# Row sums inverted by exp(-log) on ScalarE and a Newton step on VectorE, in place of VectorE's reciprocal

## The chip, the cores and the metric

The kernel runs on one core of one Trainium2 chip. A core has five engines with a queue each: TensorE (PE, matrix products; PEld is its weight load), VectorE (DVE), ScalarE (ACT), GpSimd (POOL) and SyncE (SP, which issues the DMAs here). An engine takes its own instructions strictly in order. The metric is the device time of one launch in microseconds (us), the median of several runs.

## The reference

One layer of a hybrid encoder is applied with the same weights to a group of 2048 tokens and one of 512. What matters here is the attention: 8 query heads of width 64 share 2 key/value heads, and each query attends to all tokens of its own group.

```python
def one_block(q_blk):
    s = jnp.einsum('bkgqd,btkd->bkgqt', q_blk, k).astype(jnp.float32) * scale
    p = jax.nn.softmax(s, axis=-1)
    return jnp.einsum('bkgqt,btkd->bkgqd', p.astype(v.dtype), v)
...
mixed = jnp.concatenate([o_attn * jax.nn.silu(a_gate), o_gla * jax.nn.silu(l_gate)], axis=-1)
h = h + mixed @ w_out
```

Beside it stands a gated linear attention (two directions), then an output projection, a per-layer gate (a sigmoid of a projection of the normalised result times a projected embedding), and a final RMS norm. The softmax divides each row of exponentials by its sum; that division is what the change touches.

## The kernel before, in words

Four stages follow each other on the core. Stage 1 normalises the input and projects q, k, v. Stage 2 is the linear attention; it uses Exp and Ln on ScalarE. Stage 3 is the softmax attention and the gates. Stage 4 is the output projection, the per-layer gate and the final norm.

In stage 3 the tokens lie in five chunks of 512 (chunks 0 to 3 are the long group, chunk 4 the short one). An item of work is one chunk of queries and one head: 40 items, `items` in line 860. `head` (line 783) walks over the keys in tiles of 128: 16 tiles, or 4 for chunk 4. For each tile TensorE makes the scores into a PSUM tile `pss` (lines 816 and 817; two and later three buffers), ScalarE takes the exponential into `p` (line 818), and for each two tiles ScalarE casts `p` to half precision (`phi`, line 825) and VectorE makes the rest (`plo`, line 827); TensorE then multiplies both by v into `po` (lines 797 and 805) and sums them over keys into `pz` (line 801). At the end of a head ScalarE copies `pz` to `acc` and two instructions bring `po` to `ou` (lines 833 to 837).

Other work is woven in by hand. After each exponential of line 818, `pull` (line 926) advances five generators by a counted number of steps, inside `tc.issue_after(e.ins)`, which queues what a step issues on ScalarE behind that exponential; on the other engines the planner orders by program order and readiness. The generators are the row maxima of later items (`maxima`: products `px` of line 762, VectorE reductions of line 768, two PSUM buffers), the end of stage 2 (`fin`), the gates (`gates`: 24 products `pg` of line 728 into one PSUM buffer, a Tanh on ScalarE in line 732, then line 733 on VectorE), the row sums (`normalise`) and the stores (`combine`, `store_mixed`).

`normalise` (line 840) runs once for every two heads, 20 times. It sums `acc` over partitions with four products into a PSUM tile `pn` (line 845; the tile shares the two buffers of `px`), inverts it into `rs`, and GpSimd multiplies `ou` by `rs` (line 851). Each `yield` is one step, so each of its instructions lands behind the exponential of another key tile. `combine` then multiplies by the gate, and `store_mixed` splits and stores the result to DRAM for stage 4, which reads the chunks in order of tokens.

ScalarE has table loads among its instructions. Line 56 asks for a table by the name `natural_log_exp_and_others` at the start. The program writes out no other load; the trace holds one more, just before the first Tanh of line 732.

Of the kernel before, what the change touches and what calls it, by code (L numbers as in the profile page):

```python
# [9 lines left out]
F32 = mybir.dt.float32  # L10
# [4 lines left out]
AF = mybir.ActivationFunctionType  # L15
ALU = mybir.AluOpType
# [4 lines left out]
P = 128  # L21
# [648 lines left out]
def stage3(net, s, fin=iter(()), top=None, tail=None):  # L670
    nc, tc, d = net.nc, net.tc, net.d
    with ExitStack() as ctx:
# [4 lines left out]
        rp = pool("s3r", 1)  # L677
# [162 lines left out]
        def normalise(ou, accs):  # L840
            for _ in range(2):
                yield
            pn = ps_n_tile()
            for b in range(2):
                nc.tensor.matmul(pn[b * 64:b * 64 + 64], lhsT=two, rhs=accs[b], start=True, stop=True)  # L845
            rs = rp.tile([P, 512], F32, name="rs")
            for i in range(4):
                cs = slice(i * P, (i + 1) * P)
                nc.vector.reciprocal(rs[:, cs], pn[:, cs])  # L849
                yield  # L850
            nc.gpsimd.tensor_tensor(ou, ou, rs, ALU.mult)  # L851

        def combine(c, j, ou):
# [10 lines left out]
        nt = [4 if c == 4 else 16 for c, h in items]  # L864
# [20 lines left out]
        def all_sums():  # L885
            while True:
                if pairs:
                    c, j, ou, accs = pairs.pop(0)
                    yield from normalise(ou, accs)
                    waiting.append((c, j, ou))  # L890
                else:
                    yield True
# [302 lines left out]
```

## Time and profile before

| | |
|---|---|
| median of 3 runs | 2087.77 us (2084.49 to 2088.56) |
| profiled execution, its own time | 2088.21 us |
| its span in the profile | 2086.5 us |
| mean granted TensorE clock | 0.987 |
| reciprocals of line 849 | 80, first start 672.5 us, last start 1557.2 us |
| Tanh of line 732 | 40, first start 682.2 us, last start 1515.1 us |
| table loads | 2 |

The profile is of one execution. Busy time of an engine is the time in which it ran an instruction; TensorE's is drawn out by pipelining, as the ends of matrix products are modelled. Idle time before an instruction is put down to the instruction that ended the wait. The chain of waits is followed back from the end: at each step to what released the instruction, or to its predecessor on its engine. Stage 3 with gates runs from about 690 to 1520 us.

### The profile page before, as it was taken

What the parts mean: (1) busy time and instruction counts of PE and PEld (TensorE: products, weight loads), DVE (VectorE), ACT (ScalarE), POOL (GpSimd) and SP (SyncE); (2) the same over time, 40 slices, a digit from 0 to 9 for tenths busy, and PEclk for the clock granted to TensorE, in tenths of its full rate; (3) what the DMA queues carried; (4) which work ended last, traced back from release to release, by engine and by line L of the source; (5) the groups of instructions that cost most, each with busy time, mean ns of one, the idle gap of its engine ahead of it and who ended that gap; (6) DMA issues with size and microseconds to landing.
All of it is one profiled execution on the core that took longest, in us unless ns stands there. A gap on an engine that the chain in (4) does not pass through costs nothing.

```text
span 2086.5 us, 29717 instructions
## 1 busy us (share of the span) xinstructions
PE 2004.7 (96%) x11174; PEld 1321.1 (63%) x11174; DVE 1332.6 (64%) x2242; ACT 1181.5 (57%) x2048; POOL 356.5 (17%) x292
## 2 busy tenths in 40 slices
PE   8999999999979999999999999999989999999998
PEld 7788887777754444444444444444437888888886
DVE  7555444665678889899889989988874222222223
ACT  5343233555558888788878878878883222222222
POOL 2434431000430011011011011100120111111111
PEclk9999999999999999999999999999999999999999
DMA  8887445666775225333333422522236222222220
GB/s 269 241 254 209 134 128 167 202 203 199 227 229 188 79 97 171 106 112 108 114 112 128 143 80 94 177 68 93 80 115 187 86 86 86 86 86 86 81 66 33
DMA packets 251360, 282.23 MB, mean 135 GB/s; under 512 B 41872, under 2 KB 180976, under 8 KB 246096
## 3 DMA queue, kind: packets, MB, share of 16 engines
q1 hardware_dynamic: 251072, 279.80, 43.0%
q8 instruction: 88, 1.44, 0.3%
q0 software_dynamic: 144, 0.52, 0.1%
q14 instruction: 56, 0.46, 0.1%
HBM read 189.64 MB, written 90.64 MB: 134 GB/s over the span
## 4 chain that ended last, share of the span: by engine, by line
PE 79%; DVE 8%; ACT 7%; DMA 3%; issue 2%; POOL 1%; SPq 0%; DVEq 0%; POOLq 0%; ACTq 0%
PE pm L108 38%; PE pg L728 9%; PE po L805 5%; PE px L762 4%; PE pss L816 4%; PE pss L817 4%; ACT p L818 3%; PE po L797 3%; PE pp L108 3%; PE pz L801 2%; DVE plo L827 2%; DVE mx L768 2%; ACT phi L825 2%; PE pn L845 1%; PE pt L1080 1%
## 5 line engine op out<-in xcount | busy, mean ns | idle before, releaser
L818 ACT ACTIVATE p<-pss,lnp,qk_scale 128x512 f32<-128x512 f32 x544 | 407.3, 781 | 113.4 <-PE pss L817 100.9
L768 DVE TENSOR_REDUCE mx<-px 128x1 f32<-128x512 f32 x544 | 357.0, 682 | 68.1 <-PE px L762 66.6
L728 PE MATMUL pg<-xt,wg 128*128 128x512 f32 x960 | 376.4, 484 | 1.1 <-DVE g L733 0.9
L827 DVE TENSOR_TENSOR plo<-p,phi 128x1024 f16<-128x1024 f32 x272 | 338.9, 1248 | 34.6 <-ACT phi L825 32.8
L825 ACT CAST phi<-p 128x1024 f16<-128x1024 f32 x270 | 283.2, 1049 | 5.6 <-PE po L805 0.9
L728 PEld LDWEIGHTS pg<-xt,wg 128*128 128x128 f32 x960 | 181.7, 190 | 69.1 <-issue 6.7
L816 PE MATMUL pss<-qa,ka 128*128 128x512 f16 x544 | 208.8, 385 | 11.1 <-ACT p L818 10.2
L762 PE MATMUL px<-ka,qa 128*128 128x512 f16 x544 | 201.0, 384 | 10.3 <-DVE mx L768 6.3
L817 PE MATMUL pss<-qb,kb 66*128 66x512 f16 x544 | 206.4, 383 | 0.3 <-ACT qb L781 0.3
L1128 DVE SCALAR_TENSOR_TENSOR th<-th,pp 128x512 f32<-128x512 f32 (+1 forms) x41 | 27.7, 675 | 190.0 <-ACT th L1127 190.0
L805 PE MATMUL po<-phi,v 128*128 128x512 f16 x544 | 142.5, 385 | 0.0
L108 PE MATMUL pm<-xt,wlqk 128*128 128x512 f32 x480 | 120.4, 410 | 7.8 <-DMA xt<-scr_xt 6.3
L816 PEld LDWEIGHTS <-ka 128*128 128x128 f16 x544 | 52.8, 97 | 107.0 <-issue 83.7
L1081 ACT CAST hT<-pt 128x512 fp32r<-128x512 f32 x40 | 23.5, 587 | 169.7 <-PE pt L1080 169.7
L108 PEld LDWEIGHTS pm<-xt,wlqk 128*128 128x128 f32 x480 | 94.3, 199 | 30.0 <-DMA xt<-scr_xt 7.5
L108 PE MATMUL pm<-wq_h,xt 128*128 128x512 f32 x320 | 103.2, 403 | 4.5 <-ACT xt L203 4.3
L762 PEld LDWEIGHTS <-qa 128*128 128x128 f16 x544 | 52.4, 98 | 83.9 <-issue 41.9
L1127 ACT ACTIVATE th<-pm,rh 128x512 f32<-128x512 f32 (+1 forms) x41 | 27.9, 680 | 133.8 <-PE pm L108 133.8
L108 PE MATMUL pm<-wpg0h,hT 128*128 128x512 f32 x320 | 101.0, 396 | 0.1
L108 PE MATMUL pm<-wo0h,mx 128*128 128x512 f32 x320 | 100.5, 395 | 0.0
L108 PE MATMUL pm<-wo1h,mx 128*128 128x512 f32 x320 | 100.4, 394 | 0.0
L851 POOL TENSOR_TENSOR ou<-ou,rs 128x512 f32<-128x512 f32 x20 | 35.5, 1777 | 378.5 <-DVE rs L849 378.5
(250 smaller groups left out, 3866.1 us busy)
## 6 DMA issues: line engine op xcount, KB each, us to landing
wg<-scr_wg SPq DMA_DIRECT2D x40, 1024.0 KB
scr_xt<-xt SPq DMA_DIRECT2D x20, 1024.0 KB
xt<-scr_xt SPq DMA_DIRECT2D x20, 1024.0 KB
xt<-scr_xt SPq DMA_DIRECT2D x40, 512.0 KB
scr_mx<-hl SPq DMA_DIRECT2D x40, 512.0 KB
mx<-scr_mx SPq DMA_DIRECT2D x20, 1024.0 KB
x<-x_prompt SPq DMA_DIRECT2D x27, 512.0 KB
scr_wg<-wghl SPq DMA_DIRECT2D x32, 256.0 KB
```

The source lines that it names most:

```text
L108: self.nc.tensor.matmul(out, lhsT=a[k], rhs=b[k], start=first and i == 0, stop=last and i == n - 1)
L728: nc.tensor.matmul(ps, lhsT=w[:, wi, k], rhs=xi, start=i == 0, stop=i == 23)
L762: nc.tensor.matmul(ps, lhsT=q[0][:, b * P:(b + 1) * P], rhs=ks[ti][0][:, h // 4], start=True, stop=True)
L768: nc.vector.tensor_reduce(mx[:, b, i:i + 1], product(i, b), axis=AX.X, op=ALU.max)
L797: nc.tensor.matmul(po[r:r + 32], lhsT=ks[t // 4][2][:, t % 4 + i, kv, g * 32:g * 32 + 32], rhs=lo[:, i], start=t == 2, stop=False)
L801: nc.tensor.matmul(pz[i * 32:i * 32 + 32], lhsT=ones, rhs=(lo, hi)[i // 2][:, i % 2], start=t == 2, stop=t + 4 == n)
L805: e = nc.tensor.matmul(po, lhsT=ks[t // 4][2][:, t % 4 + i, kv], rhs=hi[:, i], start=False, stop=t + i + 1 == n)
L816: nc.tensor.matmul(ps, lhsT=ka[:, kv, cs], rhs=q[0], start=True, stop=False)
L817: nc.tensor.matmul(ps, lhsT=kb[0:66, kv, cs], rhs=q[1][0:66], start=False, stop=True)
L818: e = nc.scalar.activation(p[:, i], ps, AF.Exp, bias=net.lnp, scale=net.qk_scale)
L825: nc.scalar.copy(hi, p)
L827: nc.vector.tensor_tensor(lo, p, hi, ALU.subtract)
```

## The change

The reciprocal of `pn` was taken by VectorE in four pieces of 128 columns, one per step. Now ScalarE takes the logarithm of all 512 columns into a new SBUF tile `nt`, then in the next step exp(-nt) into `rs`; VectorE makes nt = -pn * rs in the third step and rs = (nt + 2) * rs in the fourth, one Newton step for the reciprocal. The number of steps is the same. The pool `rp` holds one more tile of 128 x 512.

```diff
--- before.py
+++ after.py
@@ -843,11 +843,17 @@
             pn = ps_n_tile()
             for b in range(2):
                 nc.tensor.matmul(pn[b * 64:b * 64 + 64], lhsT=two, rhs=accs[b], start=True, stop=True)
+
             rs = rp.tile([P, 512], F32, name="rs")
-            for i in range(4):
-                cs = slice(i * P, (i + 1) * P)
-                nc.vector.reciprocal(rs[:, cs], pn[:, cs])
-                yield
+            nt = rp.tile([P, 512], F32, name="nt")
+            nc.scalar.activation(nt, pn, AF.Ln)
+            yield
+            nc.scalar.activation(rs, nt, AF.Exp, scale=-1.0)
+            yield
+            nc.vector.scalar_tensor_tensor(nt, pn, -1.0, rs, ALU.mult, ALU.mult)
+            yield
+            nc.vector.scalar_tensor_tensor(rs, nt, 2.0, rs, ALU.add, ALU.mult)
+            yield
             nc.gpsimd.tensor_tensor(ou, ou, rs, ALU.mult)
 
         def combine(c, j, ou):
```

## Rows read from the trace of the kernel before

**Rows 1.** The page's part 1: busy time, share, instructions of each engine.

```profile
PE 2004.7 (96%) x11174; PEld 1321.1 (63%) x11174; DVE 1332.6 (64%) x2242; ACT 1181.5 (57%) x2048; POOL 356.5 (17%) x292
```

**Rows 2.** Busy time by stretch; first row shown names the columns.

```profile
core 0: us, PE busy (x) PEld busy (x) DVE busy (x) ACT busy (x) POOL busy (x), PEclk, DMA share, GB/s
690.00:1520.00 830.00, 817.16 (x4967) 373.38 (x4966) 732.99 (x1001) 683.34 (x906) 94.13 (x56) 1.00 0.33 111
```

**Rows 3.** The chain of waits, 690 to 1520 us, by line.

```profile
by line: PE pg L728 20.8%; PE po L805 12.1%; PE px L762 10.2%; PE pss L816 9.7%; PE pss L817 8.9%; PE po L797 6.9%; ACT p L818 6.0%; PE pz L801 5.5%; DVE plo L827 4.8%; DVE mx L768 3.1%; issue 2.9%; ACT phi L825 2.8%; PE pn L845 2.5%; PE pn
```

**Rows 4.** TensorE's waits, 690 to 1520 us: total us, times, longest.

```profile
PE pss L816 <- ACT p L818: 3.8, 12, 0.7
PE po L797 <- DVE plo L827: 3.0, 7, 0.9
PE pn L780 <- DVE mt L777: 1.6, 2, 0.9
PE px L762 <- DVE mx L768: 1.5, 5, 0.6
PE pg L728 <- DVE g L733: 0.9, 2, 0.7
```

**Rows 5.** Groups of VectorE instructions by line, whole span.

```profile
L849 DVE RECIPROCAL rs<-pn 128x128 f32<-128x128 f32 x80 | 72.5, 932 | 1.8 <-PE pn L845 1.4
...
L733 DVE SCALAR_TENSOR_TENSOR g<-g,pg 128x512 f32<-128x512 f32 x40 | 27.1, 678 | 1.1 <-ACT g L732 0.8
```

**Rows 6.** The reciprocal line by itself: who waited for it (us, times).

```profile
  POOL ou L851: 378.5, 19
```

**Rows 7.** Groups of ScalarE instructions by line, whole span.

```profile
L732 ACT ACTIVATE g<-pg 128x512 f32<-128x512 f32 x40 | 23.7, 591 | 2.7 <-PE pg L728 2.6
...
L455 ACT ACTIVATE l<-l,one 128x512 f32<-128x512 f32 x20 | 14.4, 720 | 0.3
...
L454 ACT ACTIVATE l<-l 128x512 f32<-128x512 f32 x20 | 12.7, 637 | 0.3
...
L56 ACT ACT_TABLE_LOAD x1 | 1.3, 1283 | 0.8 <-PEq L1184 0.8
L732 ACT ACT_TABLE_LOAD x1 | 1.3, 1283 | 0.0
```

**Rows 8.** Line 732 between reciprocals: stretch, length, busy us (instructions), clock, DMA.

```profile
672.50:728.70 56.20, 3.06 (x4) 1.00 0.21 73
...
895.20:909.90 14.70, 0.60 (x1) 1.00 0.31 106
...
1504.50:1554.70 50.20, 0.59 (x1) 0.90 0.40 129
```

**Rows 9.** ScalarE in order of time: start, length, instruction, idle before.

```profile
679.36 1.58 ACT L818 ACTIVATE p<-pss,lnp,qk_scale 128x512 f32<-128x512 f32 x2
680.95 1.28 ACT L732 ACT_TABLE_LOAD   x1
682.25 0.60 ACT L732 ACTIVATE g<-pg 128x512 f32<-128x512 f32 x1
682.74 1.04 ACT L825 CAST phi<-p 128x1024 f16<-128x1024 f32 x1
683.68 2.13 ACT L818 ACTIVATE p<-pss,lnp,qk_scale 128x512 f32<-128x512 f32 x3
```

**Rows 10.** TensorE in order of time, the same stretch.

```profile
682.04 0.38 PE L817 MATMUL pss<-qb,kb 66*128 66x512 f16 x1
682.69 0.62 PE L797 MATMUL po<-plo,v 128*32 128x512 f16 x8 [0.27 <-DVE plo L827]
```

**Rows 11.** The row-sum tile: the products that fill it.

```profile
L845 PE MATMUL pn<-acc,two x80: 592/643/1116, 670.1 to 1553.6; 128*64 128x512 f32 x80
```

**Rows 12.** Timeline at the end of attention, columns as in group 9.

```profile
1556.64 1.15 ACT L99 ACTIVATE wo1h<-wstage 128x512 fp32r<-128x512 f32 x2
...
1565.92 0.63 PE L108 MATMUL pm<-wo1h,mx 128*128 128x512 f32 x2
```

## The prediction

> **What bounds the kernel now.** I read the page first and stayed with TensorE, which is busy for 96% of the span [rows 1]. Then I read busy time by stretch, because the change lies in attention alone. From 690 to 1520 us, where the gates are woven in, TensorE is busy for 817.16 of 830 us (98%), VectorE for 732.99 (88%) and ScalarE for 683.34 (82%) [rows 2]. The chain of waits of that stretch says the same: its five longest entries are TensorE's, VectorE's `plo` and `mx` hold 4.8% + 3.1% = 7.9%, ScalarE's `p` and `phi` 6.0% + 2.8% = 8.8%, and the reciprocal is not among the entries shown [rows 3]. Last, TensorE's own waits: it waits 3.8 us for `p` and 3.0 + 1.6 + 1.5 + 0.9 = 7.0 us for VectorE, out of 830 [rows 4]. So TensorE is the bound, VectorE and ScalarE follow closely, and relief of VectorE has little left to give.
>
> **What is removed.** 80 reciprocals of 932 ns take 72.5 us of VectorE [rows 5]. Only GpSimd ever waited for them [rows 6], and GpSimd is 17% busy [rows 1].
>
> **What is added on VectorE.** 40 instructions on 128x512 with three operands. The nearest row, the gate's in line 733, takes 678 ns [rows 5], so 27.1 us come back and VectorE is freed of 72.5 - 27.1 = 45.4 us. In the stretch lie 18 of the 20 inversions, and VectorE goes to 733.0 - 72 x 0.932 + 36 x 0.678 = 690.3 us, 83%. As 7.9% of the chain is VectorE's, I value the relief at 0.079 x 45.4 = 3.6 us gained. It can't be less than nothing, and in the stretch not more than all of TensorE's idle time, 830 - 817.2 = 12.8 us.
>
> **What is added on ScalarE: the functions.** A Ln that reads PSUM is not in the trace. Tanh on the same shape out of PSUM takes 591 ns, the Ln of stage 2 (with a bias column) 720, its Exp 637 [rows 7]. I take 0.59 + 0.64 = 1.23 us, times 20 = 24.6 us (27.1 with the 720). By ScalarE's share of the chain that is 0.088 x 24.6 = 2.2 us; the bounds are 0 and 27.1.
>
> **What is added on ScalarE: table loads.** This decides. The trace has two loads of 1283 ns. The first one serves the Exp and the Ln of stage 2. The second stands before the first Tanh of line 732, so the first table has no Tanh; after it all Exp and Tanh run without another load [rows 7]. A table with all three would have needed no second load. So a Ln of `normalise` that comes after a Tanh needs a load, and the Tanh or the Exp after it needs another to go back. The first inversion, at 672.5 us, is before the first Tanh and needs none. In the 19 stretches from one inversion's start to the next there is always a Tanh: four instructions of line 732 in the first (one is the load), a single one in the shortest of 14.7 us, and one in the last [rows 8]. That makes 19 x 2 = 38 loads more, 48.8 us of ScalarE. Whether the load back comes at the next Exp (when Ln's table has no Exp) or at the next Tanh does not change the count. I take it at the next Exp: a choice made for the Ln alone need not look further.
>
> With 18 x (1.23 + 2.57) = 68.3 us more in the stretch, ScalarE goes to 751.6 us, 91%. It is then above VectorE, but still under TensorE.
>
> What does a load cost TensorE? The one load inside attention shows it. The exponentials before it end at 680.94, load, Tanh and cast follow, and the next exponential starts at 683.68, a gap of 2.74 us [rows 9]. TensorE filled it with three pairs of score products, the last at 682.04, and then stood 0.27 us for `plo` [rows 10]. With load, Ln and load between two exponentials the gap is 1.28 + 0.59 + 1.28 = 3.15 us, 0.41 more; if a cast falls between them, which cost 683.68 - 682.74 = 0.94 there, it is 4.09 us, 1.35 more. So TensorE stands for 0.27 + 0.41 = 0.68 to 1.62 us per inversion, 19 times: 12.9 to 30.8 us. The far bounds are 0 (all filled) and 48.8 us (both loads exposed whole). I take 12.9, because in the row the gate products could not fill the gap (their PSUM buffer waited for that very Tanh), while around a Ln they mostly can.
>
> The Trainium skill ("ScalarE: Activation LUTs", section "What ACT_TABLE_LOAD costs") gives the same 1283 ns but adds a drain of about 1380 ns, some 2.66 us per switch. The trace disagrees on the drain: the load starts 0.01 us after the last exponential ends and the Tanh 0.02 us after the load [rows 9]. By the page's figure ScalarE would lose 38 x 2.66 = 101 us (an estimate from that page).
>
> **What is added as a wait.** Ln stands in ScalarE's queue in the step in which `pn` is filled, and behind it is the next exponential of `p`, for which the scores' buffers and `plo` wait. VectorE waited only 1.4 us in all for these products [rows 5], so I price it at nothing; if each Ln waited for one of the longest of them it would be 20 x 1.1 = 22 us [rows 11].
>
> **What is moved.** The four instructions keep the four steps, no DMA moves, `pn` is given back a step earlier. I cost that at nothing. The last inversion stands at the start of stage 4, where ScalarE's 3.8 us go among casts of weights: the last cast of that half starts at 1556.64 and TensorE reads it from 1565.92 [rows 12], some 8 us of cover; without it, 3.8 us.
>
> **The sum.** 12.9 + 2.2 - 3.6 = 11.5 us. The profiled execution took 2088.2 us, 0.4 above the median, so 2099.7 against it and 2099.3 against the median.
>
> **The rivals.** A difference of 0.2%, 4.2 us, is about what a measurement can tell.
>
> - *ScalarE sets the pace; slower by much.* Each burst empties the scores' buffers and the gates' one PSUM buffer, and both loads come out whole: 48.8 + 2.2 - 3.6 = 47.4, 2135 us. For it: 91% with bursts of over 3 us. Against it: 9% of idle time remains, and the load in the trace cost 0.27 of its 1.28 us.
> - *Idle time around each load too.* An engine that stood for another load's length, 1.38 us, at each load would add 2.76 to the 0.68 us: 19 x 3.44 + 2.2 - 3.6 = 64, 2152 us. The idle time of 0.0 before the load speaks against it [rows 7]. It is the drain that the Trainium skill's page on ScalarE states.
> - *Hidden; no change.* TensorE's order is made anew with the longer ScalarE work in it, gate products are drawn forward, and loads cost under 5 us in all: 2084 to 2092 us. To this belongs the case that the second table serves Ln as well, without any load: 2.2 - 3.6 = -1.4, 2086 us. No Ln runs after 681 us, so the rows alone do not rule it out.
> - *Faster.* VectorE is what TensorE waits for more often (7.0 against 3.8 us [rows 4]); freed, it brings `plo` and `mx` earlier and the 7.0 us go: 2.2 - 7.0 = -4.8, 2083 us, at most 2.2 - 12.8 = -10.6, 2077 us. It decides only where the 38 loads cost under 0.6 us together, as every microsecond of them comes off.
>
> **How the numbers follow.** Forecast (2092 to 2112 us) 0.46; ScalarE the pace 0.13; idle around loads 0.03; hidden 0.20 and no loads 0.03; faster 0.15. Slower by over 0.2% is then 0.62, within 0.23, faster 0.15. The predicted time is 2099 us. The range is 2084 to 2126: the upper end is 30.8 + 2.2 and a quarter of the 22 us of waiting, 38 above; the lower takes in the hidden case. Outside lie most of the faster case and the upper part of the two slow ones.
>
> **What would show it.** Right: about 40 loads on ScalarE instead of 2, 40 instructions of 0.6 us for Ln and Exp, VectorE at 83% and ScalarE at 91% in the stretch, and TensorE's waits for `p` and `plo` grown from 6.8 us by some 13. Wrong: two loads only; or 40 loads with TensorE's idle time in the stretch still near 13 us; or ScalarE's idle time nearly gone, which would be the first rival.

## The result and the profile after

The changed kernel took 2117.22 us (median of 4 runs, 2115.5 to 2121.69), the kernel before 2086.86 beside it. The ratio is 1.0151, 95% interval 1.0136 to 1.0166: 31.5 us slower (28.4 to 34.6). Here and below such a difference is the ratio's excess over 1 times the median of the kernel before; the two medians differ by 30.4 us. The prediction had the sign and the loads as the cause, but 11.5 us: 2099 us, with 2092 to 2112 as its likeliest case. The profiled execution took 2115.5 us with a span of 2113.5.

Part 1 of the page, and busy time by stretch, answer to [rows 1, 2]. The last Tanh of line 732 now starts at 1537.8 us and not at 1515.1, so the second stretch of 852 us holds about the work that 830 us held before.

```profile
PE 2010.0 (95%) x11174; PEld 1322.5 (63%) x11174; DVE 1302.0 (62%) x2202; ACT 1250.5 (59%) x2126; POOL 349.4 (17%) x292
```

```profile
690.00:1520.00 830.00, 803.39 (x4853) 366.83 (x4855) 687.49 (x943) 725.80 (x951) 83.44 (x53) 1.00 0.32 108
...
690.00:1542.00 852.00, 822.30 (x4962) 374.90 (x4961) 704.49 (x966) 744.97 (x975) 88.11 (x56) 1.00 0.32 108
```

Over the 852 us ScalarE is 87% busy, VectorE 83%. TensorE's idle time went from 12.8 us to 29.7, so 16.9 of the stretch's 22 us more are idle TensorE.

A closer pair of stretches runs from the first product of line 845 to the start of the last, with the same work of TensorE in it; first before, then after:

```profile
670.10:1553.60 883.50, 861.15 (x5240) 390.41 (x5241) 772.47 (x1051) 725.23 (x964) 97.56 (x58) 0.99 0.33 110
```

```profile
668.80:1574.80 906.00, 868.07 (x5242) 392.52 (x5241) 743.17 (x1012) 789.47 (x1037) 90.67 (x58) 0.99 0.32 107
```

So of the 27.0 us between the two spans 22.5 lie in attention: 15.6 of TensorE's idle time and 6.9 of time that is drawn as busy. Another 5.1 lie at the start of stage 4: from the last product of line 845 to the first product `pp` (the projected embedding) it took 27.3 us before and 32.4 after.

ScalarE's groups answer to [rows 7]: out<-in, shape, count, busy us, mean ns, idle time before. Line 849 is the Ln, 851 the Exp.

```profile
L849 ACT ACT_TABLE_LOAD x19 | 24.4, 1283 | 0.3
...
L818 ACT ACT_TABLE_LOAD x10 | 12.8, 1283 | 0.2
L851 ACT ACTIVATE rs<-nt 128x512 f32<-128x512 f32 x20 | 12.5, 624 | 0.1
L849 ACT ACTIVATE nt<-pn 128x512 f32<-128x512 f32 x20 | 12.0, 598 | 0.7 <-PE pn L845 0.5
L851 ACT ACT_TABLE_LOAD x9 | 11.5, 1283 | 0.2
L56 ACT ACT_TABLE_LOAD x1 | 1.3, 1283 | 0.8 <-PEq L1190 0.8
L732 ACT ACT_TABLE_LOAD x1 | 1.3, 1283 | 0.0
```

These are 40 loads, as forecast: one before each Ln but the first, and one back before the next Exp, which is an exponential of line 818 in 10 cases and the inversion's own Exp in 9. VectorE's two new instructions (lines 853 and 855) took 2% and 9% more than the 678 ns forecast:

```profile
L855 DVE SCALAR_TENSOR_TENSOR rs<-nt,rs 128x512 f32<-128x512 f32 x20 | 14.8, 741 | 0.2
L853 DVE SCALAR_TENSOR_TENSOR nt<-pn,rs 128x512 f32<-128x512 f32 x20 | 13.8, 691 | 28.8 <-ACT rs L851 28.7
```

So the price of every added instruction was near. What was wrong is what they cost the path. TensorE's waits in the 852 us (total us, times, longest) answer to [rows 4]:

```profile
PE pss L816 <- ACT p L818: 11.6, 17, 2.1
PE px L762 <- DVE nt L853: 4.8, 10, 1.0
PE px L762 <- DVE mx L768: 4.8, 11, 0.9
PE pg L728 <- DVE g L733: 4.1, 4, 1.4
PE po L797 <- DVE plo L827: 2.2, 7, 0.4
PE pn L780 <- DVE mt L777: 0.9, 1, 0.9
```

The wait for `p` trebled from 3.8 us. The wait for `px` behind line 853 is new: the row sums share their two buffers with `px` and are now given back only after the loads. One burst, one of the two dearest, shows it, first ScalarE's timeline, then TensorE's (start, length, instruction, idle before):

```profile
1186.62 0.68 ACT L836 ACTIVATE ou<-po,vinv 64x512 f32<-64x512 f32 x1 [0.37 <-PE po L805]
1187.32 1.28 ACT L849 ACT_TABLE_LOAD   x1
1188.62 0.60 ACT L849 ACTIVATE nt<-pn 128x512 f32<-128x512 f32 x1
1189.23 1.28 ACT L818 ACT_TABLE_LOAD   x1
1190.53 0.78 ACT L818 ACTIVATE p<-pss,lnp,qk_scale 128x512 f32<-128x512 f32 x1
...
1193.33 0.59 ACT L732 ACTIVATE g<-pg 128x512 f32<-128x512 f32 x1
```

```profile
1188.44 1.05 PE L728 MATMUL pg<-xt,wg 128*128 128x512 f32 x3
...
1190.21 0.38 PE L817 MATMUL pss<-qb,kb 66*128 66x512 f16 x1
1191.36 0.38 PE L816 MATMUL pss<-qa,ka 128*128 128x512 f16 x1 [0.76 <-ACT p L818]
...
1192.60 0.39 PE L762 MATMUL px<-ka,qa 128*128 128x512 f16 x1 [0.44 <-DVE nt L853]
1193.20 0.38 PE L762 MATMUL px<-ka,qa 128*128 128x512 f16 x1 [0.20 <-DVE mx L768]
...
1194.33 0.62 PE L797 MATMUL po<-plo,v 128*32 128x512 f16 x8 [0.25 <-DVE plo L827]
```

Load, Ln and load hold ScalarE from 1187.32 to 1190.51, and TensorE stands four times behind it: for a score buffer, for the row sums' buffer, for a reduction, for `plo`; 1.65 us together. In [rows 10] it stood once, for 0.27. This is not the average: in the 7 us from the start of Ln's load TensorE is idle for 0 to 2.26 us in the 18 bursts within attention, 12.9 us in all, 0.72 each. That is little more than half of the 22.5 us.

### The profile page after: what moved, and what is told of

It is laid out like the page before. It is cut to its first block, busy times and chain, and to the rows that moved or that the text cites. A ratio compares the mean times of both kernels' runs of the same rounds, so it can differ in the third digit from the quotient of the medians.

```text
span 2113.5 us, 29742 instructions
## 1 busy us (share of the span) xinstructions
PE 2010.0 (95%) x11174; PEld 1322.5 (63%) x11174; DVE 1302.0 (62%) x2202; ACT 1250.5 (59%) x2126; POOL 349.4 (17%) x292
## 4 chain that ended last, share of the span: by engine, by line
PE 72%; ACT 11%; DVE 9%; DMA 3%; issue 3%; POOL 1%; SPq 0%; DVEq 0%; POOLq 0%; ACTq 0%
PE pm L108 37%; PE pg L728 7%; PE po L805 4%; PE px L762 4%; ACT p L818 4%; PE pss L816 4%; PE pss L817 3%; PE po L797 3%; PE pp L108 2%; DVE mx L768 2%; DVE plo L827 2%; PE pz L801 2%; ACT phi L825 2%; PE pt L1086 1%; ACT L849 1%
## 5 line engine op out<-in xcount | busy, mean ns | idle before, releaser
L728 PE MATMUL pg<-xt,wg 128*128 128x512 f32 x960 | 367.8, 477 | 4.3 <-DVE g L733 4.1
L827 DVE TENSOR_TENSOR plo<-p,phi 128x1024 f16<-128x1024 f32 x272 | 345.0, 1269 | 32.8 <-ACT phi L825 31.6
L728 PEld LDWEIGHTS pg<-xt,wg 128*128 128x128 f32 x960 | 180.5, 190 | 80.5 <-DVE g L733 12.5
L108 PE MATMUL pm<-xt,wlqk 128*128 128x512 f32 x480 | 115.5, 398 | 6.4 <-DMA xt<-scr_xt 4.9
L108 PE MATMUL pm<-wpg1h,hT 128*128 128x512 f32 (+1 forms) x336 | 99.4, 379 | 0.0
```

Source lines behind the costliest of these rows:

```text
L108: self.nc.tensor.matmul(out, lhsT=a[k], rhs=b[k], start=first and i == 0, stop=last and i == n - 1)
L728: nc.tensor.matmul(ps, lhsT=w[:, wi, k], rhs=xi, start=i == 0, stop=i == 23)
L827: nc.vector.tensor_tensor(lo, p, hi, ALU.subtract)
```

## The experiments

The theory after the result: the 38 loads are the whole loss, because a long piece in ScalarE's queue delays everything that hangs on it. The rivals: ScalarE's added functions and the longer-held buffer cost most; or the loss lies in single places that can be mended. All runs were timed beside the kernel before, in the order in which they stand here.

**No loads.** In the changed kernel, Square for Ln (so that the result is no longer an inverse):

```diff
-            nc.scalar.activation(nt, pn, AF.Ln)
+            nc.scalar.activation(nt, pn, AF.Square)
```

> The changed kernel with Square in place of Ln, so the logarithm is left out and the inverse is not one; all else stays, and no table has to be switched. My theory: the 38 extra table loads and their place in ScalarE's queue are the whole loss, so the trace has 2 loads and the time falls back to 2084 to 2089 us (before: 2087, changed kernel: 2117). Rival, the added work as such: two more 128x512 functions per inversion on ScalarE and the row-sum buffer held until the Newton step cost most of the 30 us, loads hide; then 2100 us or more.

Measured: 2085.9 us, 1.0006 (0.9994 to 1.0017), 1.3 us slower than before (-1.3 to 3.5), with two loads:

```profile
L851 ACT ACTIVATE rs<-nt 128x512 f32<-128x512 f32 x20 | 12.5, 627 | 0.2
L849 ACT ACTIVATE nt<-pn 128x512 f32<-128x512 f32 x20 | 11.9, 597 | 7.1 <-PE pn L845 7.1
...
L56 ACT ACT_TABLE_LOAD x1 | 1.3, 1283 | 0.8 <-PEq L1190 0.8
L732 ACT ACT_TABLE_LOAD x1 | 1.3, 1283 | 0.0
```

The loss is gone with the loads, though both functions and the Newton step stay. Functions and relief of VectorE together are worth nothing measurable.

**Loads only.** In the kernel before, one short Ln per inversion:

```diff
             rs = rp.tile([P, 512], F32, name="rs")
+            one = rp.tile([P, 1], F32, name="one_ln")
+            nc.scalar.activation(one, net.one, AF.Ln)
```

> The kernel before, with VectorE's four reciprocals, and one added Ln of a single column (128x1, of a constant) in each inversion's first step: it brings the same 38 loads and nearly no other work. My theory: 40 loads in the trace, 1.0 to 1.5 us lost per inversion, so 2106 to 2117 us. Rival, the added work as such: under 2095 us, with the loads filled by other work of TensorE.

Measured: 2109.63 us, 1.0122 (1.0108 to 1.0137), 25.4 us slower (22.5 to 28.6); 40 loads; the short Ln takes 203 ns. That is 25.4 / 19 = 1.34 us per pair (1.18 to 1.5). The last Ln waits for nothing and was issued at 1534.6 us, still within attention.

**The last inversion by VectorE.** In the changed kernel (`done` counts the inversions):

```diff
+            done.append(1)
+            if len(done) == 20:
+                for i in range(4):
+                    cs = slice(i * P, (i + 1) * P)
+                    nc.vector.reciprocal(rs[:, cs], pn[:, cs])
+                    yield
+            else:
...
```

> The changed kernel with the last of the 20 inversions made by VectorE's reciprocal as before; 38 loads in the trace. My theory: of the loss about 5 us come from this one inversion, because its loads delay the weight casts that stage 4 starts with; the first projected-embedding product then waits about 3 us and not 8.9, and the time is 2111 to 2113 us. Rival: the longer wait at the start of stage 4 comes from DMAs that all started later; then the time stays at 2117 us within 2.

Measured: 2110.9 us, 1.0127 (1.0114 to 1.014), 26.5 us slower than before (23.8 to 29.2), so 5 us better than the changed kernel, at the edge of what the intervals tell apart. The wait that I had named moved less than I said. It is the first projected-embedding product's wait at the start of stage 4; here is TensorE's row of the kernel before, of the changed kernel and of this one:

```profile
PE pp L108 <- ACT pT L1081: 3.2, 1, 3.2
```

```profile
PE pp L108 <- ACT pT L1087: 8.9, 1, 8.9
```

```profile
PE pp L108 <- ACT pT L1096: 6.2, 1, 6.2
```

Without loads (Square) it was 6.2 us as well. And in the two kernels with a plain copy (below), whose last inversion is as before, it was 7.8 and 9.2 us:

```profile
PE pp L108 <- ACT pT L1087: 7.8, 1, 7.8
```

```profile
PE pp L108 <- ACT pT L1087: 9.2, 1, 9.2
```

So this wait does not go with the loads of the last inversion alone, and that the 5 us are theirs is not shown.

**Row sums copied first.** In the changed kernel, Ln and Newton step then read `pc`:

```diff
+            pc = rp.tile([P, 512], F32, name="pc")
+            nc.vector.tensor_copy(pc, pn)
-            nc.scalar.activation(nt, pn, AF.Ln)
+            nc.scalar.activation(nt, pc, AF.Ln)
```

> The changed kernel with the row sums first copied to SBUF by VectorE (20 copies more, 12 us of VectorE), so that their PSUM buffer comes free before the loads and not after them. My theory: the row-maxima products no longer wait for the Newton step (4.8 us in the changed kernel), and 3 to 5 us are won: 2112 to 2114 us. Rival: the buffer is not what these products really wait for (ScalarE's late exponentials are), and the time stays at 2117 us or rises by up to 2.

Measured: 2119.48 us, 1.0175 (1.0153 to 1.0196), 36.5 us slower than before (31.9 to 40.9): no gain. TensorE's waits, 690 to 1542 us:

```profile
PE pss L816 <- ACT p L818: 11.7, 18, 1.8
PE px L762 <- DVE mx L768: 10.1, 16, 1.5
```

The 4.8 us for line 853 are gone, and the wait for `mx` grew from 4.8 to 10.1. My theory on this point fell. Either the shared buffer was only where the lateness showed, or the 20 copies on VectorE cost what it gave back; the run does not tell these apart.

**Loads apart, in the changed kernel.** Ln's table asked for by name:

```diff
+            nc.scalar.preload_act_table_set("natural_log_exp_and_others")
             nc.scalar.activation(nt, pn, AF.Ln)
```

> The changed kernel with the table that holds both Exp and Ln asked for by name before each Ln: the number of loads stays 40, but the load back comes at the next Tanh and no longer at the next Exp, so two loads never stand between two exponentials. Theory A (bunching: a gap between exponentials of up to about 2.7 us is covered, the rest is lost): the loss in attention falls from 23 us to about 10, 2098 to 2105 us. Theory B (every microsecond of ScalarE counts the same, wherever it stands): 2113 to 2119 us, as the changed kernel.

Measured: 2107.88 us, 1.0096 (1.0079 to 1.0112), 20.0 us slower than before (16.5 to 23.4). Most loads back now stand before a Tanh:

```profile
L849 ACT ACT_TABLE_LOAD x19 | 24.4, 1283 | 0.3
L732 ACT ACT_TABLE_LOAD x18 | 23.1, 1283 | 0.3
...
L850 ACT ACT_TABLE_LOAD x1 | 1.3, 1283 | 0.0
L852 ACT ACT_TABLE_LOAD x1 | 1.3, 1283 | 0.0
```

One of the 18 is the first Tanh's own, as before. The last inversion, behind the last Tanh, kept both its loads, one before its Ln (line 850) and one before its Exp (line 852), with a cast between. Neither theory had the time: place matters, for some 11 us, but loads apart are far from free.

**Relief only.** In the kernel before, the inversion left out:

```diff
-            for i in range(4):
-                cs = slice(i * P, (i + 1) * P)
-                nc.vector.reciprocal(rs[:, cs], pn[:, cs])
-                yield
+            nc.vector.tensor_copy(rs, pn)
+            for _ in range(4):
+                yield
```

> The kernel before with the inversion left out (row sums are copied to rs by one VectorE copy per inversion, no reciprocal, ScalarE as before): VectorE is freed of about 60 us. The price used in the prediction, 7.9% of VectorE's time: 4 to 5 us won, 2081 to 2083 us. Theory no relief (TensorE is the bound, VectorE's waits are taken over by others): 2084 to 2088 us. Rival, VectorE is what TensorE waits for: 2076 to 2080 us.

Measured: 2086.95 us, 0.9996 (0.9984 to 1.0008): -0.8 us (-3.3 to 1.7). VectorE's busy time on the page fell by 39 us (1332.6 to 1293.5), less than the 60 that the prices of reciprocal and copy give. TensorE still waits 3.9 us for `plo` and 2.7 for `mx`, while VectorE waits longer for TensorE's `px` (690 to 1520 us, before and here):

```profile
DVE mx L768 <- PE px L762: 60.6, 90, 2.1
```

```profile
DVE mx L768 <- PE px L762: 92.1, 138, 2.4
```

Freeing VectorE buys nothing here.

**One load, and two loads in different steps.** In the kernel before; the second kernel has the line in the steps i = 0 and i = 2 of the reciprocal's loop:

```diff
+            if 1 < len(done) < 20:
+                nc.scalar.preload_act_table_set("exp_and_others")
             for i in range(4):
...
```

> The kernel before with one needless load of the table already in use in the first step of 18 of the 20 inversions (not the first, not the last): 20 loads in the trace, nothing else added. Theory A (bunching): a single load of 1.28 us costs what the one in the trace of before cost, 0.27 us each, so 4 to 6 us: 2089 to 2092 us. Theory B (every microsecond of ScalarE counts the same): half of what the pair costs, 10 us: 2094 to 2098 us.

> The kernel before with two needless loads per inversion, one in the first and one in the third step (18 of the 20 inversions): 38 loads in the trace, always with exponentials between them. Theory A (bunching): 36 times 0.27 to 0.35 us, so 2095 to 2099 us. Theory B (every microsecond of ScalarE counts the same): as with the pair in one step, 20 us, 2104 to 2109 us.

Measured: one load 2097.81 us, 1.0048 (1.0035 to 1.0061), 10.0 us (7.3 to 12.7), which is 0.56 us for each of 18 loads. Two loads 2100.24 us, 1.0068 (1.0052 to 1.0083), 14.2 us (10.9 to 17.3), 0.39 for each of 36. The single load fits theory B's time and is above A's 4 to 6 us. Two apart lie between the two theories' times, clearly under the 25.4 us of the pair in one step. A's 0.27 us was idle time of TensorE behind a load, and as such it was not too small: in the 7 us from each of the 18 single loads TensorE is idle for 1.6 us in all, 0.09 each, while the attention took 7.6 us longer than before. Most of the price does not show as idle time behind the load.

**A plain copy in the load's place.** In the kernel before, n = 10 and n = 24:

```diff
+            if 1 < len(done) < 20:
+                idle = rp.tile([P, n, P], F32, name="idle")
+                nc.scalar.copy(idle, net.ident.unsqueeze(1).broadcast_to([P, n, P]))
             for i in range(4):
...
```

> The kernel before with one useless copy of 128x1280 on ScalarE (estimated 1.3 us, from the 1064 ns that line 193 takes for 128x1024) in the first step of 18 inversions, and no load: the place and length of the single load, without a load. Theory: a load is nothing but ScalarE's time, so the same 10 us as the single load, 2094 to 2100 us. Rival: a load costs more than its 1283 ns (what follows it starts late, or the engine is drained), so a plain copy of that length costs under 5 us, below 2092 us.

> The same with a copy of 128x3072 (estimated 2.8 us: load, a short Ln and load in one piece) in 18 inversions. Theory A (bunching: the longer the piece, the dearer each microsecond): at least as much as the pair of loads in one step, 20 to 28 us, 2107 to 2116 us, which is more than twice the copy of 1.3 us. Theory B (every microsecond the same): 2.2 times the copy of 1.3 us. Rival (loads are special): under 15 us, below 2102 us.

The copies' lengths (ns, smallest, median, largest), of the first and of the second kernel:

```profile
L852 ACT COPY idle<-ident x18: 1246/1266/1292, 727.2 to 1505.6; 128x1280 f32<-128x1280 f32 x18
```

```profile
L852 ACT COPY idle<-ident x18: 2739/2762/2789, 730.5 to 1519.6; 128x3072 f32<-128x3072 f32 x18
```

Measured: 2097.99 us, 1.0052 (1.0036 to 1.0068), 10.9 us (7.5 to 14.2); and 2113.07 us, 1.0123 (1.0103 to 1.0143), 25.7 us (21.5 to 29.8). Within the intervals the copy of 1.27 us costs what the load of 1.28 costs, and the one of 2.76 us what the pair costs: no sign that a load is more than ScalarE's time. The longer copy costs 2.4 times the shorter one at 2.2 times the length, which fits what either theory said. The profiled executions are less even: in attention the copies cost 4.6 and 16.7 us, the single load 7.6 and the pairs 18.8, and the copies' kernels lost 5.1 and 6.0 us more at the start of stage 4, where no copy stands. Single executions scatter by some 3 us: attention took 22.5 us more in the changed kernel and 25.3 in that with the last inversion by VectorE, whose products there stand in the same order.

**Both mends.** The changed kernel with loads apart and the last inversion by VectorE:

> The changed kernel with both mends at once: the table that holds Exp and Ln asked for by name before each Ln (so that the load back comes at the next Tanh), and the last inversion by VectorE's reciprocal. If the two losses are separate they add: 11 us (loads apart) and 5 us (the last inversion) off the changed kernel's 30, so 14 to 16 us over before, about 2101 to 2104 us. If the loads' place does not matter once the last inversion is mended: 2110 to 2113 us. Faster than before (under 2084 us) only if the freed VectorE is worth something after all.

Measured: 2103.65 us, 1.0085 (1.0068 to 1.0103), 17.7 us (14.2 to 21.5). That is 2.3 us under loads apart alone (20.0) where 5 would be the sum: the intervals hold that the two add, and also that the last inversion is worth nothing. None of the experiments points to a kernel with these loads that is faster than before.

## Why the prediction was off

- **Number and length of the loads, Ln, Exp, the two VectorE instructions: right.** 40 loads of 1283 ns; 598, 624, 691 and 741 ns. VectorE's busy time fell by 30.6 us on the page (1332.6 to 1302.0) and not by 45.4; other instructions of VectorE took longer, and why is not shown.
- **Price of the loads: the step that failed.** "12.9 to 30.8 us ... I take 12.9, because ... around a Ln they mostly can [fill]." The mechanism was right, a burst in ScalarE's queue that leaves TensorE without work, and so was the span of prices; the term taken from it was half of the price. Loads alone cost 25.4 us: 1.34 us per inversion against the 0.68 taken. The 0.68 was TensorE's idle time behind the burst, and as that it was near: 0.72 on average in the changed kernel. But idle time behind the burst is not the price. Attention grew by 22.5 us with 12.9 us of it, and with single loads by 7.6 us with 1.6. The rest is idle time elsewhere and TensorE's time drawn as busy.
- **What filled the gap.** In [rows 10] two pairs of score products and two `px` lie in the gap; the third pair had started before it, at 680.42. In the changed kernel gate products covered a part: 12 ran in the burst from 784.33 on, three in the one shown above. These ended a group of 24, and the next group began only at 1197.30, as the Tanh that reads their buffer stood behind the burst too (1193.33).
- **The row sums' buffer: "given back a step earlier", at nothing.** In time it comes later, after the loads, and TensorE waited 4.8 us for it; what that cost is open, as the copy to SBUF won nothing.
- **Relief of VectorE: 3.6 us credited, none found.** With the reciprocals left out the time moved by -0.8 us (-3.3 to 1.7). VectorE's share of the chain was no price: freed, it waited longer for `px` (92.1 us against 60.6).
- **The two functions: 2.2 us, near enough.** Together with the relief they came to 1.3 us.
- **The last inversion: costed at nothing under "8 us of cover".** It may have cost about 5 us by the times, 2.3 by the pair with loads apart; neither is clear of noise. I looked at the first read of the cast weights and not at the loads of further weights, which wait for free staging buffers.
- **The sum by measured terms:** 25.4 + 1.3 + 5.0 = 31.7 us, against 31.5 measured. Each term is known to some 3 us and the last is not shown, so that they meet this closely is luck. What is clear of noise is the 12.5 us by which the term for loads was too small.
- **The signs named.** ScalarE came to 87% of the stretch and not 91%, and TensorE's waits for `p` and `plo` grew by 7.0 us (6.8 to 13.8) and not by 13; other waits grew beside them.
- **The rivals.** ScalarE did not set the pace: over the 852 us it still had 107 us of idle time. Idle time around each load (the second rival, whose 1.38 us is no load's length: a load took 1.28) did not appear: 0.3 us before 19 loads. On this the Trainium skill ("ScalarE: Activation LUTs", section "What ACT_TABLE_LOAD costs") has a drain of about 1380 ns per switch; the trace shows none here, as Ln starts 0.02 us after its load. Its section "Table sets: the hidden batching unit" counts one load for Ln followed by Exp; here the trace has a load between them, and none where the shared table was asked for by name, but for the last inversion.
- **Still open:** why most of the price does not show as idle time behind the piece, and why pieces of different length and place cost from 0.3 to 0.5 us per us of ScalarE. One rival was not tested: the planner orders TensorE's products anew in each kernel. Of the 5608 products of attention 2983 stand in the same place before and after, and 4138 in the changed kernel and in the one with Square. So no run tells what the load itself costs from what another order costs.

## What to carry to other kernels

An engine with 18% of idle time is not free to take a burst: what counts is how long the piece stands in the queue between two instructions that others wait for. In this kernel such a piece cost 0.3 to 0.5 of its length. The idle time that the bounding engine shows behind a piece is not its price: here it was a sixth of what single loads cost and about half of what the bursts cost. Add the piece alone to the kernel and compare the times. Before a function goes to ScalarE, see which functions run between two of its uses, and count the table loads.

## What the runs showed of the hardware

A table load behaved as 1.28 us of plain ScalarE work, as far as the intervals tell: in the same place a copy of 1.27 us cost 10.9 us (7.5 to 14.2) over 18 inversions and a load 10.0 (7.3 to 12.7), and the next instruction started 0.02 us after the load. With Square for Ln, 24.4 us of ScalarE work in pieces of 0.6 us, beside a relieved VectorE, cost 1.3 us (-1.3 to 3.5), while 23 us in pieces of 1.28 us cost 10.
